# A transformer block on eight cores: a new opening order, later denominator transfers, and GpSimd's Newton steps in pieces

## The chip, the cores and the metric

The kernel runs on all eight cores of one Trainium2 chip. Each core computes one of the eight sequences, with the same instructions, and the cores exchange nothing. Cores 0 to 3 are die 0, cores 4 to 7 die 1, as the profile's list of cores groups them. The metric is the device time of the slowest core in microseconds, us below. Some executions fall into a second, slower state in which one die, sometimes both, shows a lower granted TensorE clock: in the fourth run of the changed kernel cores 4 to 7 show 0.816 to 0.821 and take 3669.6 to 3689.8 us, cores 0 to 3 show 0.985 to 0.99 and take 3208.5 to 3237.1. Such runs are named slow. One execution of each kernel was recorded by the profiler, and its trace gives every core.

TensorE does the matmuls (PE in the profile, PEld for its weight loads), VectorE is DVE, ScalarE is ACT, GpSimd is POOL. SPq is the DMA queue that SyncE issues from. It works in order. On core 5 of the kernel before it issued nothing from 834.4 to 852.80 us, when GpSimd's product `s_ao` had just ended (at 852.77); the store of that product went out then, the load of q behind it at 853.23, and TensorE waited 7.5 us for that q.

## The reference, cut to what matters

```python
h = rms_norm(x, norm1_g) * (1.0 + sc1) + sh1          # x: 4096 x 1024 per core
q, k, v, f_logit, glu_in, gate_logit = split(h @ w_in)
q, k = rms_norm per head of 64 (16 heads)
log_f = log_sigmoid(f_logit + b_forget)
branch_a = forgetting_attention(q, k, v, log_f) @ w_attn_proj      # causal softmax with a decay bias
u = glu_in[..., :1024] * sigmoid(glu_in[..., 1024:])
u = causal_depthwise_conv(u, conv_w, conv_b)                       # 31 taps
branch_b = silu(layer_norm(u)) @ w_conv_proj
merged = sigmoid(gate_a) * branch_a + sigmoid(gate_b) * branch_b
x = x + g1 * (merged @ w_out)
x = x + g2 * (square(relu(h2 @ w_mlp1)) @ w_mlp2)                  # h2: normed and modulated x
```

## The kernel before

The names in the profiles: `s_P` are the exponentials and `p_pS` the scores that they are made of; `s_qT` is a tile of q; `s_dg` are the diagonal matrices of the convolution and `s_us` its tiles of u, read back from the DRAM tensor `ucr`; `s_ysq` are squares for LayerNorm's statistics; `s_Vo` is the scaled V; `s_xn` is a normalised block of x and `s_hT` its transpose.

The kernel has four stages: an opening that computes the modulation and starts the projections (0 to 180 us), the rest of the projections to q, k and v (to about 485 us), attention with the whole convolution branch woven into it (to about 1935 us), and the gates, the output projection and the MLP. A helper records every operation with what it reads and writes, and puts in the waits; inside the engines the order is the order of recording. So the program text decides in which order each engine meets its work.

**Opening.** The modulation row is gathered in `macc` by VectorE. WQ and WK are loaded by GpSimd's queue after it, and name `macc` as something they read, so that WV, which lies on `macc`'s memory, must wait until they have landed:

```python
DMA("pool", WQ[...], wq_d[...], [b_macc], [], d_wq[half], dwrites=[b_WQ[half]])     # both halves, then WK
...
DMA("pool", WV[...], wv_d[...], [], [b_WV[half]], d_wv[half])                       # lies on macc
...
for b in range(4):
    norm1(b)            # ScalarE: sum of squares; VectorE: scale; DVE (b < 4) or GpSimd: shift
    if b >= 1:
        norm2(b - 1)    # TensorE: 8 transposes; ScalarE: copy into hT
norm2(3)
for t in range(NT):     # tiles of 512 rows; tile 0 goes Q, K, V one after another, the others Q K V Q K V ...
    ...
```

**Attention.** 288 groups, each of one key tile of 512 against one query tile of 512 for two heads. A group gives ScalarE four exponentials of 128x1024 and VectorE the scaled V. Half units of the convolution branch are put into the middle of a group, and what is to follow later is put off with `later(us, fn)`, which counts on a clock that the program keeps while it is written: two ticks of 2.2 "model us" for each group, one at its start and one at its end.

```python
def tick(us):                       # run what has come due
    clock[0] += us
    ...
for gi in range(NG + 1):
    tick(2.2)                       # the group's start tick
    ...                             # q_load(i + 2) at the first group of a query tile
    emit_S(gi, 0); emit_exp(gi, 0); emit_S(gi, 1); emit_exp(gi, 1)
    ...                             # half units of the convolution branch
    for p in posts: p()             # their follow-up work: the middle of the group
    posts.clear()
    emit_S(gi, 2); emit_exp(gi, 2); emit_S(gi, 3); emit_exp(gi, 3)
    ...                             # values of the group before, scaled V, masks
    tick(2.2)                       # the group's end tick
```

**The end of a query tile.** The softmax denominators cross the partitions by way of DRAM, in five steps, each put off from the one before:

```python
later(1.5, s0)     # s0: write the sums (Dc -> dscr)
later(6.5, s1)     # s1: read them back reordered (dscr -> dcm), then later(8.5, s2)
# s2 (GpSimd): add, power -1 -> rcm; later(1.0, write rcm -> rscr); later(8.0, s3)
# s3: read back broadcast (rscr -> rb), then later(8.5, s4)
# s4 (GpSimd): ao = Oc * rb; later(1.5, store ao -> aos)
```

**LayerNorm of the convolution branch.** After the second statistics unit of a tile, GpSimd works out the reciprocal root by three Newton steps, thirteen operations in one go, and the eight chunks follow at fixed times:

```python
for it in range(3):
    ...                                                       # four operations of GpSimd
TT(lnM[:], lnM[:], lnY[:], ALU.mult, ..., eng="pool")
for c in range(KC):
    later(18.0 + 4.4 * c, lambda c=c: ln_chunk(t, c))

def ln_chunk(t, c):
    ...                                                       # the STT of an earlier chunk
    TT(z, y, lnY, mult); TT(z, z, lnM, subtract); TS(z, z, g, b)          # VectorE
    act = [lambda: ACT(th, z, Tanh)]                                      # ScalarE
    ...
    later(2.2, lambda: posts.append(mid))                                 # mid() emits the tanh
```

## Time and profile before

Three runs of the kernel before took 3327.37 to 3339.7 us, median 3335.44. The profiled execution took 3332.45 us.

| what | value | where |
|---|---|---|
| span of the eight cores | 3283.4 to 3330.8 us, median 3306 | list of cores |
| start of attention | 481.6 to 489.1 us, median 484.7 | first matmul into p_pS, per core |
| length of attention | 1408 to 1448.5 us, median 1421 | to the first matmul of the stage after it |
| the rest | 1391 to 1400 us | per core |
| TensorE's idle time in attention, core 5 | 1448.0 - 1289.8 = 158 us | windows |

Two lines of this profile were not read closely for the prediction, and they turned out to carry the result. The first is from the list of what each engine waited for, here ScalarE on core 5 in attention. The columns are the engine, what it was about to make and at which line, what it waited for, then total us, times, longest us. `s_lt` is the tanh of LayerNorm, `s_z` its input from VectorE:

```profile
ACT s_lt L363 <- DVE s_z L370: 63.3, 31, 5.7
```

ScalarE stood 63 us, 31 times, before a tanh whose input was not finished. The second view is the timeline of the same core inside one of those times (start, duration, engine, what, and in brackets the idle time before it with what ended it):

```profile
676.30 0.55 DVE L370 TENSOR_SCALAR s_z<-s_z,s_lngc,s_lnbc 128x512 f32<-128x512 f32 x1
...
676.99 0.63 ACT L363 ACTIVATE s_lt<-s_z 128x512 f32<-128x512 f32 x1 [5.72 <-DVE s_z L370]
...
678.01 3.54 ACT L363 ACTIVATE s_P<-p_pS 128x1024 bf16<-128x1024 f32 x4
...
679.17 0.61 PE L348 MATMUL p_pS<-s_qT,s_kT 64*128 64x512 bf16 x2 [3.56 <-ACT s_P L363]
```

ScalarE idles 5.72 us, until VectorE's third operation on z ends at 676.85. The tanh starts 0.14 us later, the exponentials behind it only then, and TensorE waits 3.56 us for one of them to free its scores' buffer. The exponentials had nothing to do with z; they only stood behind the tanh in ScalarE's order, the first of them at 678.01.

### The profile page before, as it was taken

What the parts mean: (1) busy time and instruction counts of PE and PEld (TensorE: products, weight loads), DVE (VectorE), ACT (ScalarE), POOL (GpSimd) and SP (SyncE); (2) the same over time, 40 slices, a digit from 0 to 9 for tenths busy, and PEclk for the clock granted to TensorE, in tenths of its full rate; (3) what the DMA queues carried; (4) which work ended last, traced back from release to release, by engine and by line L of the source; (5) the groups of instructions that cost most, each with busy time, mean ns of one, the idle gap of its engine ahead of it and who ended that gap; (6) DMA issues with size and microseconds to landing.
All of it is one profiled execution on the core that took longest, in us unless ns stands there. A gap on an engine that the chain in (4) does not pass through costs nothing.

```text
span 3330.8 us, 57506 instructions; the slowest of 8 cores (3283.4 to 3330.8 us)
## 1 busy us (share of the span) xinstructions
PE 3062.4 (92%) x23196; PEld 1478.6 (44%) x23196; DVE 1796.6 (54%) x3692; ACT 1654.0 (50%) x2458; POOL 634.3 (19%) x679
## 2 busy tenths in 40 slices
PE   2899989889798988889898999998999999999999
PEld 1455533223232332323333344444666666666666
DVE  5567664474746565473847463664444444444443
ACT  2555557778687777777787821222222222222222
POOL 0212201332323232242424120000001001000000
PEclk8999999999899999999999999999999999999999
DMA  9566457777577868867686654667011111110110
GB/s 222 129 167 164 126 157 140 161 143 162 102 141 137 152 120 134 156 121 164 125 171 142 145 174 129 196 207 244 32 39 52 38 39 39 51 39 33 58 33 26
DMA packets 274757, 400.58 MB, mean 120 GB/s; under 512 B 75829, under 2 KB 205109, under 8 KB 265529
## 3 DMA queue, kind: packets, MB, share of 16 engines
q1 hardware_dynamic: 237658, 275.13, 32.3%
q0 software_dynamic: 36832, 121.76, 19.3%
q8 instruction: 183, 3.00, 0.4%
q14 instruction: 84, 0.69, 0.1%
HBM read 347.80 MB, written 118.31 MB: 140 GB/s over the span
## 4 chain that ended last, share of the span: by engine, by line
PE 68%; DMA 13%; ACT 6%; DVE 6%; SPq 3%; POOL 3%; issue 2%; DVEq 0%; POOLq 0%; ACTq 0%
PE p_po L348 13%; PE p_ph L348 13%; PE p_pC L348 9%; PE p_pF L348 9%; PE p_pmm L348 8%; PE p_pS L348 5%; ACT s_P L363 4%; PE p_pO L348 4%; PE p_pw L348 3%; SPq L344 3%; DMA rscr<-s_rcm 2%; PE p_pD L348 2%; DMA s_dg<-dgs 2%; DMA ucr<-s_u 1%; DMA s_WK<-wk 1%
## 5 line engine op out<-in xcount | busy, mean ns | idle before, releaser
L363 ACT ACTIVATE s_P<-p_pS 128x1024 bf16<-128x1024 f32 (+3 forms) x1152 | 1022.9, 953 | 279.0 <-PE p_pS L348 261.9
L363 ACT ACTIVATE s_rl<-p_ph 128x256 f32<-128x256 f32 x512 | 192.2, 381 | 726.0 <-PE p_ph L348 716.1
L348 PE MATMUL p_pS<-s_qT,s_kT 64*128 64x512 bf16 (+3 forms) x2304 | 382.1, 375 | 112.1 <-ACT s_P L363 91.3
L374 DVE TENSOR_TENSOR s_aT<-s_rl 128x256 bf16<-128x256 f32 x512 | 242.5, 483 | 412.3 <-ACT s_rl L363 392.3
L348 PEld LDWEIGHTS p_pS<-s_qT,s_kT 64*128 64x128 bf16 x2304 | 89.5, 94 | 415.7 <-ACT s_P L363 272.0
L348 PE MATMUL p_pF<-s_hT,s_glw 128*128 128x512 bf16 x1024 | 264.2, 396 | 0.9 <-DVE s_pb L369 0.8
L374 POOL TENSOR_TENSOR s_xl<-s_xl,s_ot 128x512 f32<-128x512 f32 x60 | 79.9, 1341 | 885.6 <-DVE s_ot L374 884.4
L348 PE MATMUL p_pO<-s_P,s_Vo 128*64 128x512 bf16 x1792 | 239.5, 389 | 5.5 <-DVE s_Vo L374 5.3
L363 ACT ACTIVATE s_tha<-p_pC 128x512 f32<-128x512 f32 x128 | 75.5, 596 | 250.8 <-PE p_pC L348 186.0
L348 PE MATMUL p_pF<-s_us,s_dg 128*32 128x512 bf16 x2048 | 138.9, 402 | 23.2 <-DMA s_dg<-dgs 23.2
L374 POOL TENSOR_TENSOR s_ao<-s_Oc,s_rb 128x512 bf16<-128x512 f32 x52 | 67.3, 1295 | 468.2 <-DMA s_rb<-rscr 468.1
L348 PEld LDWEIGHTS p_pF<-s_hT,s_glw 128*128 128x128 bf16 x1024 | 90.2, 101 | 141.5 <-issue 62.9
L384 DVE TENSOR_REDUCE s_ssq<-s_sq 128x8 f32<-128x512 f32 x128 | 84.6, 681 | 115.6 <-ACT s_sq L363 115.6
L348 PEld LDWEIGHTS p_pO<-s_P,s_Vo 128*64 128x64 bf16 x1792 | 83.2, 110 | 132.7 <-issue 44.0
L348 PE MATMUL p_pD<-s_P,s_Wo 128*32 128x512 bf16 x1792 | 138.6, 386 | 0.0
L348 PE MATMUL p_pmm<-s_WQ,s_hT 128*128 128x512 bf16 x512 | 120.6, 391 | 9.7 <-ACT s_hT L363 9.6
L377 DVE SCALAR_TENSOR_TENSOR s_u<-s_th,p_pF 128x512 bf16<-128x512 f32 x64 | 43.8, 684 | 152.3 <-PE p_pF L348 152.2
L348 PE MATMUL p_pF<-s_y,s_wcp 128*128 128x512 bf16 x512 | 124.5, 380 | 0.0
L348 PE MATMUL p_pC<-s_aol,s_wap 128*128 128x512 bf16 x512 | 121.0, 379 | 2.4 <-DVE s_t L377 2.1
L374 DVE TENSOR_TENSOR s_Vd<-s_V,s_Wd 128x256 bf16<-128x256 bf16 (+3 forms) x512 | 121.1, 281 | 2.6
L348 PE MATMUL p_pC<-s_hT,s_wgb 128*128 128x512 bf16 x512 | 121.0, 379 | 0.0
L348 PE MATMUL p_pC<-s_hT,s_wga 128*128 128x512 bf16 x512 | 120.9, 379 | 0.0
(221 smaller groups left out, 5152.6 us busy)
## 6 DMA issues: line engine op xcount, KB each, us to landing
s_us<-ucr SPq DMA_DIRECT2D x256, 135.0 KB, 6.1
s_glw<-wglus POOLq DMA_DIRECT2D x64, 512.0 KB, 8.1
s_x<-x SPq DMA_DIRECT2D x32, 512.0 KB, 9.1
s_hT<-hs POOLq DMA_DIRECT2D x16, 1024.0 KB, 9.6
s_dg<-dgs SPq DMA_DIRECT2D x64, 256.0 KB, 7.7
s_rb<-rscr SPq DMA_DIRECT2D x128, 128.0 KB, 6.7
s_wcp<-wcps POOLq DMA_DIRECT2D x64, 256.0 KB, 7.5
s_wst<-w_ada SPq DMA_DIRECT2D x32, 512.0 KB, 4.3
```

The costliest lines, as they stand in the source:

```text
L344: return P.op(q, lambda e: e.dma_start(out=out, in_=in_), reads=reads, writes=writes, dsem=dsem, dwrites=dwrites)
L348: return P.op("pe", lambda e: e.matmul(out, lhsT=lhsT, rhs=rhs, start=start, stop=stop, skip_group_check=True, **kw), reads=reads, writes= ...
L363: return e.activation(out=out, in_=in_, func=func, **kw)
L374: return P.op(eng, lambda e: e.tensor_tensor(out=out, in0=in0, in1=in1, op=op), reads=reads, writes=writes, dwrites=dwrites)
L377: return P.op("dve", lambda e: e.scalar_tensor_tensor(out=out, in0=in0, scalar=scalar, in1=in1, op0=op0, op1=op1), reads=reads, writes=wri ...
L384: return P.op("dve", lambda e: e.tensor_reduce(out=out, in_=in_, op=ALU.add, axis=AX.X), reads=reads, writes=writes, dwrites=dwrites)
```

## The change

Its intent: start the opening's matmuls earlier and keep GpSimd free there; stop transfers of the denominators from blocking the queue, and GpSimd's LayerNorm run from blocking the denominators. Instructions, bytes and arithmetic stay the same. In the diff, cut to its core:

```diff
-            STT(macc[:], w_t[:], cact[:, kc:kc + 1], macc[:], ..., [b_macc])
+            STT(macc[:], w_t[:], cact[:, kc:kc + 1], macc[:], ..., [b_macc, b_tok] if kc == KC - 1 else [b_macc])
-            DMA("pool", WQ[...], wq_d[...], [b_macc], [], ...)       # WF and WK likewise
+            DMA("pool", WQ[...], wq_d[...], [b_tok], [], ...)
-        hring = arH.ring("hT", 3, [128, KC, 512], BF16, dma=True)
+        hring = Ring([arH.t2("hT%d" % i, [128, KC, 512], BF16, 4) + (P.dsem("hT%d" % i),) for i in range(3)])   # a buffer for each block
 # squares of x blocks 0 and 1 before the modulation is ready; four x loads ahead, not three;
 # the shift of x blocks 1 and 3 goes from VectorE to GpSimd
-        for t in range(NT):
-            for u in range(12):
-                kind, bb = divmod(u, 4) if t == 0 else (u % 3, u // 3)
+        # Q of block 0..3 (first halves, follow-up held), then the held work, second halves,
+        # then Q K V over blocks 0..7 one after another
+        for t in range(2, NT):
+            for u in range(12):
+                kind, bb = u % 3, u // 3
 ...
-                    if c + 3 < KC:                                   # squares made ahead
-                        ysq(t, c + 3)
+                    if c + 4 < KC:
+                        ysq(t, c + 4)
 ...
-                    for it in range(3):
+                    def newton(it):
                         ...                                          # four operations of GpSimd
-                    TT(lnM[:], lnM[:], lnY[:], ALU.mult, ..., eng="pool")
-                    for c in range(KC):
-                        later(18.0 + 4.4 * c, lambda c=c: ln_chunk(t, c))
+                        if it == 2:
+                            TT(lnM[:], lnM[:], lnY[:], ALU.mult, ..., eng="pool")
+                            for c in range(KC):
+                                later(8.0 + 4.4 * c, lambda c=c: ln_chunk(t, c))
+                        else:
+                            later(6.6, lambda: newton(it + 1))
+                    newton(0)
 ...
-                    later(1.0, lambda: DMA("sp", rscr[sl]...))
+                    later(6.0, lambda: DMA("sp", rscr[sl]...))
-                            later(1.5, lambda: DMA("sp", aos[j, :, c, :], ...))
+                            later(8.0, lambda: DMA("sp", aos[j, :, c, :], ...))
-                    later(8.0, s3)
+                    later(18.0, s3)
-            later(6.5, s1)
+            later(11.0, s1)
 ...
-                    if i + 2 < 64:
-                        q_load(i + 2)
+                    if i + 3 < 64:
+                        q_load(i + 3)
```

## The prediction

> **What bounds the kernel now.** I read the cores first, then the busy time by stretch, then what TensorE waited for, then what the DMA queue and GpSimd waited for at the longest of those waits. TensorE is busy 92% of the span of 3330.8 us, and from 2400 us to the end it is busy 923 of 930 us, so it is the engine to follow. The change touches two stretches only: the opening (0 to 180 us) and attention (about 485 to 1935 us).
>
> The opening, from the timeline of TensorE and of GpSimd (columns: start, duration, engine, what, and in brackets the idle time before it with what ended it):
> ```profile
> 39.85 6.47 PE L348 MATMUL p_pmod<-s_macc,s_onesf 128*128 128x512 f32 x8 [39.85 <-DVE s_macc L377]
> 64.10 6.20 PE L348 MATMUL p_pmm<-s_WQ,s_hT 128*128 128x512 bf16 x16 [1.21 <-ACT s_hT L363]
> 70.96 7.07 PE L348 MATMUL p_pmm<-s_WQ,s_hT 128*128 128x512 bf16 x32
> 90.94 1.03 PE L352 MATMUL p_ptx<-s_identb,s_xn 128*128 128x128 bf16 x8 [12.92 <-POOL s_xn L374]
> 91.77 6.05 PE L348 MATMUL p_pmm<-s_WQ,s_hT 128*128 128x512 bf16 x16
> ...
> 86.79 1.74 POOL L344 DMA_DIRECT2D s_WV<-wv  x2 [42.76 <-DMA s_WK<-wk]
> 88.54 2.35 POOL L374 TENSOR_TENSOR s_xn<-s_x,s_shr 128x1024 bf16<-128x1024 f32 x1
> ```
> TensorE stops for 12.9 us because the normalised block 4 comes late; that op of GpSimd stands behind the issue of the V weights, which waits until the K weights have landed. The reason is in the code: the loads of WQ and WK name macc as something they read, and WV lies on macc's memory. Sixteen matmuls take 6.1 us after each stop and half of that (32 in 7.07 us) when TensorE runs on: a stop is paid twice.
>
> Attention, from the list of what TensorE waited for between 480 and 1937 us (total us, times, longest us), then the DMA queue's own list:
> ```profile
> PE p_pS L348 <- ACT s_P L363: 91.3, 145, 3.6
> PE p_pF L348 <- DMA s_dg<-dgs: 23.2, 8, 6.3
> PE p_pS L348 <- DMA s_qT<-qs: 16.9, 3, 7.5
> PE p_pF L348 <- DVE s_ysq L374: 10.2, 7, 2.8
> ...
> SPq L344 <- DMA rscr<-s_rcm: 199.6, 41, 13.9
> SPq L198 <- POOL s_rcm L374: 151.1, 29, 17.7
> SPq L344 <- DMA dscr<-s_Dc: 109.1, 35, 7.2
> SPq L344 <- POOL s_ao L374: 71.4, 15, 18.4
> ```
> The DMA queue stands still for 531 us in these four rows alone, always for the denominator's round trips: write the sums, read them back reordered, write the reciprocals, read them back broadcast, store the result. Each wait at its head delays whatever stands behind it, and eleven times that was a q tile or a conv diagonal that TensorE then waited for: 23.2 + 16.9 = 40.1 us. The longest case, seen in the timelines of GpSimd and of the queue:
> ```profile
> 849.58 1.40 POOL L374 TENSOR_TENSOR s_lnM<-s_lnM,s_lnY 128x512 f32<-128x512 f32 x1
> 851.48 1.29 POOL L374 TENSOR_TENSOR s_ao<-s_Ocx,s_rb 128x512 bf16<-128x512 f32 x1
> ...
> 852.80 0.33 SPq L344 DMA_DIRECT2D aos<-s_ao  x1
> 853.23 0.52 SPq L344 DMA_DIRECT2D s_qT<-qs  x1
> ```
> GpSimd had run Newton steps without a break from about 834 us; the product s_ao came after them, its store stood at the head of the queue, and q behind it. TensorE waited 7.5 us for that q.
>
> The largest row, 91 us for the exponentials, is another matter. It gathers in seven stretches of some 60 us where LayerNorm chunks run: from 660 to 720 us VectorE is busy 51.3 of 60 us and TensorE 45.1, while from 720 to 840 us it is 57 and 117 of 120. There VectorE is full, ScalarE's tanh waits for it, and exponentials wait behind the tanh. The change takes no work off VectorE.
>
> [...] 387 ns for a matmul at 64 us against 221 ns at 71 us, and a granted clock of 0.76 in the 20 us around the q stall at 863 us. [...] each read-back blocks the queue; the trace shows it as the 199.6 and 109.1 us above. [...] the Vd products of 128x256 take 582 ns from 660 to 720 us and 286 ns from 720 to 830 us. [...]
>
> **The change, part by part.**
>
> 1. Opening. WQ, WK and WV load one after another at what the queue can move: the halves of WQ landed at 55.7 and 71.4 us (issue plus 15.2 and 30.0 us), those of WK at 81.2 and 86.3. With the token, WV is issued near 47 us and is here soon after 100 us, as before, but GpSimd is free. TensorE's order becomes Q0 Q1 K0 K1 V0 V1, so V is wanted only after 130 us. The first x blocks are squared before the modulation is ready, so the first transpose can start near 48.5 us, not 52.6, and the first Q matmuls at WQ's landing, 56 us, not 64. Then, however, each block goes transpose, ScalarE copy, eight matmuls in turn: 0.6 to 1.0, 1.4, and 3.1 us cold, so four half blocks last until about 74, when the second half of WQ is there. From then VectorE paces Q: 1.9 us for a half block (the trace's rhythm from 75 to 82 us), 3.9 for a whole one (two reduces, a reciprocal, two products and a copy: 1.27 + 0.25 + 1.29 + 0.68, plus 0.4 of waiting), 1.44 for each block normalised. Four held and four second halves are 8 x 1.9 = 15, five blocks normalised 7, copies 1.4, Q1 16: started at 72, done near 111, and K can start about 3 earlier, at 108. K is 8 x 3.45 + 8 x 0.45 = 31 us, V with its transposes 8 x 3.45 + 3 = 31. Tile 2 then starts near 170 instead of 180.06 us. If VectorE keeps up better than this, TensorE's own work alone would end near 164. I take a gain of 12.
>
> 2. Transfers issued later. Model time is 4.4 us for a group that lasts about 5. The read-back of the sums now follows the write by 9.5 model us (10.7 real) instead of 5, that of the reciprocals by 12 (13.5) instead of 7, the stores wait 8 instead of 1.5 after their product. Median landings are 6 to 8 us, so nearly every such wait should find its data. Together with q three tiles ahead (30 us of lead at the short tiles, where 2 gave 15) and Newton's 17 us cut into pieces of 5 us, the queue does not stand. Of the 40.1 us I take 90%: 36.
>
> 3. The clock behind these stalls: windows 580 to 600 (0.91), 860 to 880 (0.76), 1280 to 1300 and 1400 to 1420 (0.83 each) lose 0.09 + 0.24 + 0.17 + 0.17 of 20 us = 13 us; some of it falls in idle time or would come anyway: 9.
>
> 4. Four squares made ahead instead of three: of 10.2 us about 6, with 2 of clock: 8.
>
> 5. Given back: the q stalls at 863 and 1042 us lie in stretches where VectorE is full, and an earlier TensorE meets exponentials that are not ready: minus 9.
>
> Nothing is added in instructions or bytes, and matmuls, VectorE and ScalarE work are equal. Sum for the slowest core: 12 + 36 + 9 + 8 - 9 = 56 us, which from 3332 leaves 3276. The other cores bound it from below. Core 1 has only 12.8 us of such DMA waits and a span of 3283.4; core 5 has 40.1 and 3330.8. Along that line the waits cost 1.7 us each, with the clock, and a core without any would be at 3262 before the opening and the squares are counted: 3245 after. The slowest of eight, each with some remainder, should lie between the two: 3268.
>
> **The rivals.** (a) VectorE takes over wholly: 40 us of stalls vanish and the row for exponentials grows by as much. For it: VectorE at 17 of 20 us in the LayerNorm stretches. Against: four of the larger stalls (588, 606, 1296, 1411 us, some 21 us together) lie where VectorE is half idle. It would give some 3300. (b) The opening gains nothing, as Q alone is paced by VectorE: 3280. (c) Later reciprocals hold the tiles of O: five buffers, each held 46 model us instead of 31.5, that is 10.5 groups; at the seam of short tiles five are alive at once and the sixth comes 3.5 groups later. If GpSimd is late by more than 17 us there, VectorE stops and everything with it: 3310 or more. (d) LayerNorm starts 3 model us later, and its last Newton piece can stand behind a product that waits for its DMA: VectorE would wait in order for s_lnY, which today it never does. Costs under 10 us if seen. (e) All stalls and all their half clock go on every core, and the opening ends near 164 us: 3245.
>
> **Range and chances.** 3268, within 3242 (case e) to 3298 (case a). The 2% line is 3268.7, so it is nearly even: 0.48 faster, 0.50 within 2%, 0.02 slower.
>
> **What would show it.** Right: no TensorE wait for s_xn from GpSimd in the opening; the first matmuls of tile 2 at 165 to 172 us; the rows for s_dg and s_qT under 5 us together; the queue's waits for rscr, s_rcm, dscr and s_ao under a fifth of 531 us; s_ysq under 5 us; the row for exponentials between 85 and 105 us; cores within 30 us of each other. Wrong: that row above 115 us, VectorE waiting for s_lnY or for the tiles of O, or tile 2 not before 176 us.

## The result, and the profile after

Four runs of the changed kernel took 3232.71, 3238.62, 3237.57 and 3691.32 us; the last is slow. The median is 3238.1 us against 3331.4 us. All ratios in this document are computed as the mean time of one kernel's fast runs over that of the other's of the same rounds, so they are not quite the ratio of the medians. Here the ratio is 0.9715, with a 95% interval of 0.9678 to 0.9752: faster by 2.85%, about 95 us. The predicted 3268 us was 30 us too high, and the measured time lies 4 us below the range.

| profiled executions, both fast | before | after |
|---|---|---|
| span of the eight cores | 3283.4 to 3330.8, median 3306 | 3199.8 to 3231.2, median 3219 |
| start of attention, median | 484.7 | 476.6 |
| length of attention, median | 1421 | 1348 |
| the rest, per core | 1391 to 1400 | 1390 to 1396 |

So 8 us of the gain lie before attention and some 70 in it.

**The opening.** TensorE's timeline on the slowest core, 2:

```profile
58.04 3.59 PE L352 MATMUL p_pmm<-s_WQ,s_hT 128*128 128x512 bf16 x8 [8.62 <-DMA s_WQ<-wq]
...
91.07 1.01 PE L356 MATMUL p_ptx<-s_identb,s_xn 128*128 128x128 bf16 x8 [5.17 <-POOL s_xn L378]
...
177.91 3.62 PE L352 MATMUL p_pmm<-s_WQ,s_hT 128*128 128x512 bf16 x16
```

The matmuls start at 58 us instead of 64, and the one stop of 12.9 us for the normalised block is gone. In its place stand four stops for the same tile, 11.6 us together. Tile 2 starts at 177.9 us, 2.2 us earlier than before. Most of the 8 us are won between tile 2 and attention, where the kernel before has this row on its slowest core (180 to 485 us):

```profile
PE p_pmm L348 <- ACT s_hT L363: 7.2, 6, 1.2
```

In the code, a tile of hT counted as one buffer, so the first matmuls of a tile waited for the copy of its last block. The change gives each block its own. The row is 5.5 to 7.2 us on all cores before and absent on all cores after. It is absent with the opening alone (e3 below) and back at 4.3 to 7.2 us without it (e9).

**Attention.** What TensorE waited for, core 2:

```profile
PE p_pS L352 <- ACT s_P L367: 41.2, 110, 2.0
PE p_pF L352 <- DMA s_dg<-dgs: 14.8, 7, 5.5
PE p_pO L352 <- DVE s_Vo L378: 13.2, 18, 1.9
...
PE p_pF L352 <- DVE s_ysq L378: 4.6, 4, 2.1
```

This is the surprise: the row for exponentials has fallen from 91.3 to 41.2 us, and on all eight cores from 88 to 95 down to 40.6 to 42.0. The prediction had left it between 85 and 105. The rows for q and for the diagonals have gone from 40.1 to 14.8 us, the squares from 10.2 to 4.6; the scaled V has grown from about 5 to 13.2.

ScalarE's own list and timeline, same core:

```profile
ACT s_lt L367 <- DVE s_z L374: 3.5, 5, 1.1
```

```profile
682.89 1.94 ACT L367 ACTIVATE s_P<-p_pS 128x1024 bf16<-128x1024 f32 x2 [0.56 <-PE p_pS L352]
...
683.54 0.55 DVE L374 TENSOR_SCALAR s_z<-s_z,s_lngc,s_lnbc 128x512 f32<-128x512 f32 x1
...
684.72 0.63 ACT L367 ACTIVATE s_lt<-s_z 128x512 f32<-128x512 f32 x1
...
685.24 1.94 ACT L367 ACTIVATE s_P<-p_pS 128x1024 bf16<-128x1024 f32 x2
```

The wait of 63.3 us is 3.5 us now. The third operation on z ends at 684.09, while ScalarE is still busy with two exponentials; the tanh follows them at 684.72 with its input 0.63 us old. Over the first eight chunks of one tile the gap from the end of z to the start of the tanh was 0.14 us and then seven times 0.03 us before, and 0.04 to 1.43 us after. Before seven of those eight tanhs of the kernel before, ScalarE had stood idle, for 0.50 to 5.72 us. Note how small the new gaps still are: the tanh comes a whole group of some 5 us later in ScalarE's order, as shown below, yet its input is at most 1.43 us old. VectorE now finishes z later in relation to that order, so most of the added distance is used up; how little of it would do was not tested.

The windows of the stretch with LayerNorm chunks and of the whole of attention, first before on core 5, then after on core 2 (stretch, its length, busy us with the number of instructions for PE, PEld, DVE, ACT and POOL, granted clock, DMA share, GB/s):

```profile
660.00:720.00 60.00, 45.06 (x495) 16.63 (x496) 51.29 (x112) 41.15 (x55) 26.69 (x28) 0.94 0.70 133
485.00:1933.00 1448.00, 1289.80 (x12095) 447.28 (x12091) 831.43 (x2051) 1084.84 (x1274) 431.18 (x506) 0.96 0.74 143
```

```profile
655.00:715.00 60.00, 54.17 (x572) 19.58 (x572) 51.12 (x129) 50.87 (x64) 16.02 (x18) 1.00 0.69 129
477.00:1835.00 1358.00, 1264.13 (x12096) 443.71 (x12092) 840.50 (x2051) 1084.18 (x1274) 433.65 (x505) 0.99 0.75 152
```

In the LayerNorm stretch VectorE is as busy as before, 51.1 of 60 us against 51.3, and does 129 operations in it instead of 112; TensorE does 54 us instead of 45. So VectorE was not the limit there. Over attention, TensorE's idle time falls from 158 to 94 us. Its busy time falls by another 26 us for the same number of matmuls, with the clock at 0.99 instead of 0.96. In these two traces a low clock goes with stops: after the 7.5 us without q on core 5 of the kernel before, the granted clock was 0.50 from 863.1 to 867 us and 1.00 from 868.5. Cut into windows of 20 us from 485 to 1925 us, the same core shows 0.96 to 1.00 in the 43 windows in which TensorE is busy 18 us or more, and 0.89 in the mean of the 14 in which it is busy less than 16. The changed kernel's core 2, from 477 to 1837 us, has only 3 windows of the second kind and 50 of the first.

The DMA queue, core 2:

```profile
SPq L348 <- DMA ucr<-s_u: 191.9, 39, 10.0
...
SPq L198 <- POOL s_rcm L378: 47.0, 13, 10.1
SPq L348 <- DMA dscr<-s_Dc: 45.5, 11, 9.1
SPq L348 <- DMA rscr<-s_rcm: 30.3, 7, 9.9
```

With 2.6 us for s_ao, which is not shown, the four rows of the prediction come to 125 us here and to 86 to 153 us over the cores, against 531 us before (429 to 531 us). The queue does not run without a stop, though: its wait for `ucr`, the write of u that a read-back follows at once, has grown from 85.5 to 191.9 us. Other rows have grown as well: all of the queue's waits in attention together come to 787 to 841 us per core before and still to 662 to 728 us after. The author's reading, not tested, is that a queue that is less late reaches its next wait earlier. What has changed is how often something that TensorE needs stands behind the wait: eleven waits for q or diagonals, 40.1 us, on core 5 before, and seven, 14.8 us, on core 2 after. e13 below tests the row for `ucr`.

And GpSimd in the middle of Newton steps (s_z and s_lnY are its work tiles there):

```profile
641.09 1.27 POOL L378 TENSOR_TENSOR s_lnY<-s_lnY,s_z 128x512 f32<-128x512 f32 x1
...
642.60 1.67 POOL L378 TENSOR_TENSOR s_rcm<-s_rcm,s_nonec 128x8 f32<-128x8 f32 x1
644.25 1.03 POOL L378 TENSOR_TENSOR s_z<-s_lnY 128x512 f32<-128x512 f32 x1
```

The reciprocals of the denominators now run between two Newton steps.

### The profile page after: what moved, and what is told of

Same layout as the page of the kernel before. It is cut to its first block, busy times and chain, and to the rows that moved or that the text cites. A ratio compares the mean times of both kernels' runs of the same rounds, so it can differ in the third digit from the quotient of the medians.

```text
span 3231.2 us, 57532 instructions; the slowest of 8 cores (3199.8 to 3231.2 us)
## 1 busy us (share of the span) xinstructions
PE 3035.9 (94%) x23196; PEld 1474.9 (46%) x23196; DVE 1802.1 (56%) x3690; ACT 1654.5 (51%) x2458; POOL 642.4 (20%) x681
## 4 chain that ended last, share of the span: by engine, by line
PE 74%; DMA 8%; DVE 7%; ACT 6%; SPq 2%; issue 2%; POOL 1%; DVEq 0%; POOLq 0%; ACTq 0%
PE p_ph L352 13%; PE p_po L352 13%; PE p_pF L352 10%; PE p_pmm L352 9%; PE p_pC L352 9%; PE p_pS L352 6%; PE p_pO L352 5%; ACT s_P L367 4%; PE p_pw L352 3%; PE p_pD L352 3%; SPq L348 2%; DMA s_dg<-dgs 2%; DMA ucr<-s_u 2%; DMA s_wst<-w_ada 1%; DVE s_z L378 1%
## 5 line engine op out<-in xcount | busy, mean ns | idle before, releaser
L352 PE MATMUL p_pS<-s_qT,s_kT 64*128 64x512 bf16 (+3 forms) x2304 | 375.0, 370 | 44.9 <-ACT s_P L367 41.2
L352 PE MATMUL p_pF<-s_hT,s_glw 128*128 128x512 bf16 x1024 | 253.1, 383 | 5.5 <-DVE s_y L373 4.7
L352 PE MATMUL p_pO<-s_P,s_Vo 128*64 128x512 bf16 x1792 | 238.6, 388 | 13.4 <-DVE s_Vo L378 13.2
L352 PE MATMUL p_pF<-s_us,s_dg 128*32 128x512 bf16 x2048 | 134.0, 391 | 14.8 <-DMA s_dg<-dgs 14.8
L388 DVE TENSOR_REDUCE s_ssq<-s_sq 128x8 f32<-128x512 f32 x128 | 85.2, 681 | 91.3 <-ACT s_sq L367 91.0
L378 POOL TENSOR_TENSOR s_xn<-s_x,s_shr 128x1024 bf16<-128x1024 f32 x30 | 70.4, 2348 | 287.2 <-DVE s_x L381 241.5
## 6 DMA issues: line engine op xcount, KB each, us to landing
s_hT<-hs POOLq DMA_DIRECT2D x16, 1024.0 KB, 12.5
```

The source lines that it names most:

```text
L352: return P.op("pe", lambda e: e.matmul(out, lhsT=lhsT, rhs=rhs, start=start, stop=stop, skip_group_check=True, **kw), reads=reads, writes= ...
L378: return P.op(eng, lambda e: e.tensor_tensor(out=out, in0=in0, in1=in1, op=op), reads=reads, writes=writes, dwrites=dwrites)
L388: return P.op("dve", lambda e: e.tensor_reduce(out=out, in_=in_, op=ALU.add, axis=AX.X), reads=reads, writes=writes, dwrites=dwrites)
```

## The experiments

The theory after the result: **the place of the tanh**. In the kernel before, a chunk of LayerNorm is due 18.0 model us after its statistics, and that is the end tick of a group. Its tanh is put off by 2.2, which is the next group's start tick, and it is emitted in the middle of that group: half a group behind VectorE's three operations. In the changed kernel 6.6 + 6.6 + 8.0 makes the chunk due at a start tick; 2.2 later is the end tick of the same group, and the tanh comes in the middle of the next: one and a half groups behind. Nobody asked for this; it falls out of where the numbers land between ticks. The rivals: the exponentials gained because the queue, GpSimd or the opening let VectorE run ahead; or the gain is the queue's after all and the row only shows it.

All kernels named below gave correct results.

### One part at a time

**e1_before_chunk20**: the kernel before with the chunks alone moved to the next tick.

```diff
-                        later(18.0 + 4.4 * c, lambda c=c: ln_chunk(t, c))
+                        later(20.0 + 4.4 * c, lambda c=c: ln_chunk(t, c))
```

> The kernel before with one number changed: the LayerNorm chunks are emitted 20 instead of 18 model us after the statistics, which moves them from the last tick of a group to the first tick of the next and so the tanh of a chunk from half a group to a full group behind its VectorE work. Theory (slot of the tanh): ScalarE's wait for s_z falls from about 60 us to under 8, the wait for the exponentials from 88-95 us to 40-50 on every core, and the time falls by 40 to 55 us with nothing else of the change in place. Rival (the row fell because Newton no longer blocks GpSimd and the DMA queue): both rows stay where they are and the time is within 8 us of before.

Four of its six runs were slow. The two fast ones, 3331.83 and 3301.30 us, give 0.9934 (0.9835 to 1.0032): a gain of 22 us that the interval doesn't separate from nothing. The profile fell in the slow state, with die 0 undisturbed; TensorE's waits on its core 2, in attention:

```profile
PE p_pF L348 <- DMA s_dg<-dgs: 55.3, 15, 11.4
PE p_pS L348 <- ACT s_P L363: 39.5, 105, 2.0
PE p_pS L348 <- DMA s_qT<-qs: 25.9, 5, 10.9
PE p_pO L348 <- DVE s_Vo L374: 19.1, 23, 1.9
```

One number in the program, and the exponentials' row is 39 to 41 us on all cores, as in the changed kernel, with ScalarE's wait for z at 0.7 to 3.4 us. (By the ticks the tanh is now one and a half groups behind, not the full group of the expectation.) So the place of the tanh makes the row. But less time is won than the row gave back: on the cores of die 0 the diagonals now cost 36 to 55 us and q 7 to 26. The queue is the next limit close behind, by these waits. The row for the scaled V rises too, from about 5 us to 14 to 19 on all cores.

The undisturbed dies tell more than the interval. Over the eight undisturbed dies of the six runs the slowest core took 3309 us in the mean, over the twelve of the kernel before in the same rounds 3333 us (standard errors 5 and 3): 24 us less. The gain is there, and about half of the 40 to 55 us expected.

**e2_after_chunk10**: the same the other way, in the changed kernel.

```diff
-                                later(8.0 + 4.4 * c, lambda c=c: ln_chunk(t, c))
+                                later(10.0 + 4.4 * c, lambda c=c: ln_chunk(t, c))
```

> The changed kernel with 8 made 10 in the same place: the chunks go back to the last tick of a group, two model us later, with Newton in pieces and all other parts kept. Theory (slot of the tanh): the wait for s_z comes back to 50-65 us, the exponentials' row to 80-95 us, and the time rises by 35 to 55 us over the changed kernel. Rival (Newton in pieces, or the free queue, did it): rows and time stay within 8 us of the changed kernel.

Two fast runs of four, 3293.05 and 3273.5 us; 0.9834 (0.9756 to 0.9911). The changed kernel loses 0.0119 of the ratio, 40 us, by this number alone. Waits of TensorE and of ScalarE on core 2, from 480 to 1890 us:

```profile
PE p_pS L352 <- ACT s_P L367: 79.6, 136, 3.4
```

```profile
ACT s_lt L367 <- DVE s_z L374: 54.1, 29, 4.0
```

The row is back (78 to 86 us over the cores, each in its whole attention), with ScalarE's wait beside it (49 to 57 us), and the scaled V is down again at 6 to 10 us. What the chunk's later time does besides, by 2.2 model us, is separated from the tanh's place in e7 below.

**e3_before_opening**: the kernel before with the changed opening only.

```diff
 # the hunks of the change up to the projections of tile 2 and later: token, per-block buffers,
 # early squares, held first halves, order Q0 Q1 K0 K1 V0 V1; attention is that of the kernel before
```

> The kernel before with the opening alone of the change (order, per-block buffers, token, early squares); attention as before. Theory: the first attention matmul comes about 8 us earlier on the median core, attention is as long as before (median 1420 us), and the time falls by 6 to 12 us. Rival (the parts multiply: a core that starts attention earlier meets other DMA traffic): attention changes by over 10 us either way.

Three fast runs of five, 3337.08 to 3345.12 us; 1.0007 (0.996 to 1.0053). Attention starts at 469.5 to 480.7 us, median 479, so a few us earlier, and takes 1407 to 1467 us. The interval is 15 us wide to each side and can't show a gain of 8. The waits for q and diagonals were 6 to 49 us per core, median 29, which seemed high; the run of the kernel before further down shows that they vary as much there.

**e4_before_transfers**: the kernel before with the four later times only.

```diff
-                    later(1.0, lambda: DMA("sp", rscr[sl]...))
+                    later(6.0, lambda: DMA("sp", rscr[sl]...))
-                            later(1.5, lambda: DMA("sp", aos...))
+                            later(8.0, lambda: DMA("sp", aos...))
-                    later(8.0, s3)
+                    later(18.0, s3)
-            later(6.5, s1)
+            later(11.0, s1)
```

> The kernel before with the four later issue times of the denominator's transfers alone. Theory: the queue's waits for rscr, s_rcm, dscr and s_ao fall below 250 us from 531, TensorE's waits for s_dg and s_qT together to 5-15 us a core from a median of 18, the exponentials' row stays at 85-95 us, and the time of the slowest core falls by 15 to 30 us. Rival (the queue's waits were the whole cause, the exponentials included): the exponentials' row falls below 60 us and the time by over 50 us.

Four fast runs, 3314.93 to 3325.41 us; 0.9947 (0.9908 to 0.9986): 18 us. The queue's four rows fall to 106 to 135 us per core, and q and diagonals have a median of 15 us (18 in the first profile of the kernel before, 38 in the second), while the exponentials stay at 84 to 90. So later transfers work, alone, for less than the predicted 36 us with their companions, and don't touch the exponentials. The rival that the queue's relief freed ScalarE falls here.

### Two parts together, and the tanh apart from the chunk

**e11_before_chunk20_transfers**: e1 and e4 in one kernel, five numbers of the kernel before.

```diff
 # later(18.0 -> 20.0) for ln_chunk, and the four times of e4
```

> The kernel before with two parts joined that each gave only 0.5 to 0.7% alone: the chunks at 20 model us, and the four later issue times of the denominator's transfers. Theory (two bounds close behind each other, TensorE's wait through the exponentials and the DMA queue; taking one away exposes the other): the exponentials' row 40-45 us, s_dg and s_qT together under 20 us on the median core, and the time 65 to 85 us under before, more than the two single gains together (about 40). Rival (the gains only add): 35 to 45 us.

Four fast runs, 3272.55 to 3284.69 us; 0.9838 (0.9796 to 0.9879), about 54 us. This lies between the two expectations. The two parts alone gave 22 and 18. That together they give more than the sum is not shown, as e1's interval alone is wider than the difference. The row is 40 to 41 us and the queue's four rows 142 to 177 us, but diagonals still cost 21 to 41 us on the cores: the long Newton run is still there.

**e7_after_chunk10_tanh44**: the chunks where e2 has them, and the tanh put off longer, so that it again comes one and a half groups behind.

```diff
-                                later(8.0 + 4.4 * c, lambda c=c: ln_chunk(t, c))
+                                later(10.0 + 4.4 * c, lambda c=c: ln_chunk(t, c))
-            later(2.2, lambda: posts.append(mid))
+            later(4.4, lambda: posts.append(mid))
```

> The changed kernel with the chunks back at the last tick of a group (10 for 8, which cost some 40 us) but the tanh posted 4.4 instead of 2.2 model us after its chunk, so one and a half groups later. Theory (it is the distance of the tanh from its VectorE work, not the place of that work): ScalarE's wait for s_z under 5 us, the exponentials' row at 35-50 us, the time within 12 us of the changed kernel. Rival (the place of the chunk's VectorE work in the group is what counts): the row stays near 82 us and the time 35 us or more above the changed kernel.

Three fast runs of four, 3225.9 to 3237.75 us; 0.9691 (0.9641 to 0.974). The row is 41 to 43 us, ScalarE's wait for z 0 to 1.2. With the chunks at the slow time, the tanh's distance alone brings everything back. So it is the distance between VectorE's z and ScalarE's tanh, not the time of the chunk. Whether it is also a little better than the changed kernel the intervals don't tell.

**e9_after_old_opening**: the changed kernel with the opening of before.

```diff
 # the hunks of the opening undone; attention is that of the changed kernel
```

> The changed kernel with the opening of before. Alone the opening gave nothing. Theory (its 8 us were swallowed in attention because the queue bounded there; in the changed kernel the queue is free): the first attention matmul 8 us later than in the changed kernel, attention as long, time 5 to 12 us above the changed kernel. Rival (the opening is worth nothing in either): within 3 us.

Three of five runs were slow, and no interval was made of the two fast ones, 3252.06 and 3249.55 us. Their mean over that of the kernel before in the same rounds is 3250.8 / 3339.4 = 0.9735, 7 us worse than the changed kernel. Attention starts at 481 to 489 us and takes 1339 to 1368 us, as long as in the changed kernel within its spread (1333 to 1360). So in these traces the opening's part is its earlier end; two fast runs cannot show more.

**e8_after_late_dg**: two new ideas on top of the changed kernel. TensorE stops once for 12.8 us near the start of the MLP, for a relu of ScalarE, and after it the granted clock is 0.50 from 2234.7 to 2240 us, 0.95 in the 5 us after that and then 1.00. The code suggests why: six late weight loads name a buffer of VectorE's squares as read, so that VectorE may not write it again until they have landed, and the relu's buffers fill up. It is the same false chain as macc's in the opening, and the same token should undo it. And the diagonal is issued ahead of the four u loads of the same convolution unit.

```diff
+        b_late = Buf()
-                    TT(a_t[:], r_t[:], r_t[:], ALU.mult, [r_b], [a_b])
+                    TT(a_t[:], r_t[:], r_t[:], ALU.mult, [r_b], [a_b, b_late] if tt == 0 and f == 3 else [a_b])
-                        late.append(a_b)
+                        late.append(b_late)
+            DMA("sp", d_t[:]..., dgs[c], ...)      # before the loop of four u loads, not after it
```

> The changed kernel with two small repairs: the loads of the last MLP weights read a token instead of the activation tile (the same repair as the opening's; today the tile's next writer waits until the loads have landed and TensorE stops for 12.8 us), and a conv diagonal is loaded ahead of the four pieces of u that must wait for their own round trip. Theory: the 12.8 us stop goes with its half clock, s_dg falls from 1-20 us to under 5 but some moves to s_us; 12 to 22 us under the changed kernel, near 3220. Rival (the stop is the weights' own landing): the stop stays, now named by the weights, and the time is within 5 us of the changed kernel.

Three fast runs of four, 3223.84 to 3234.51 us; 0.9683 (0.9635 to 0.9732), 11 us better than the changed kernel with overlapping intervals. The stop of 12.8 us is 0.9, and the part after attention takes 1381 us instead of 1394. The diagonals wait 0 us, but the u tiles behind them wait 3 to 19 us instead: that part only moved the wait.

### The remaining parts, taken out of the changed kernel

**e10_after_whole_newton**: Newton in one go again, with the chunks at the tick that keeps the tanh's place.

```diff
-                    def newton(it):                      # pieces, 6.6 apart, chunks at 8.0
+                    for it in range(3):
                         ...
+                    for c in range(KC):
+                        later(20.0 + 4.4 * c, lambda c=c: ln_chunk(t, c))
```

> The changed kernel with Newton's thirteen steps in one piece again, the chunks kept at the first tick of a group (20 model us). Two parts of before joined (chunks and transfers) had still shown 21 to 41 us of waits for s_dg and 1 to 13 for s_qT a core. Theory (the unbroken Newton holds GpSimd 17 us and with it the reciprocals and the queue; the pieces remove this): s_dg back to 15-30 us on the median core, exponentials' row still 40-45, time 12 to 30 us above the changed kernel. Rival (q three tiles ahead and the squares made the difference): s_dg under 12 us on the median core, time within 6 us of the changed kernel.

Four fast runs of five, 3265.9 to 3268.7 us; 0.9796 (0.9747 to 0.9846). The pieces are worth 0.0081 of the ratio, 27 us. TensorE's waits on core 2:

```profile
PE p_pF L352 <- DMA s_dg<-dgs: 43.4, 10, 10.7
```

Diagonals wait 17 to 43 us per core, against 1 to 20, and no other row of TensorE's grew, the one for exponentials being 39 to 42 us: the cost shows in the diagonals, by way of the queue.

**e12_after_q2_ysq3**: q two tiles ahead and three squares ahead, as before.

```diff
-                    if i + 3 < 64:            # q_load
+                    if i + 2 < 64:
-                    if c + 4 < KC:            # ysq
+                    if c + 3 < KC:
```

> The changed kernel with q two tiles ahead and three squares made ahead, as before. Theory (the q part is hidden once the queue is free, the squares cost 5 us): s_qT under 5 us a core, s_ysq back to about 10 us from 5, time 4 to 12 us above the changed kernel. Rival (q three ahead carries the gain in the queue): s_qT over 8 us on the median core and the time 15 to 30 us above.

Three fast runs of four, 3238.34 to 3254.56 us; 0.9741 (0.9671 to 0.981): 9 us, less than the intervals. In the trace the squares' row is 10 to 13 us instead of 5, and q waits 0 to 4.6 us instead of 0.

**e13_best**: an attempt to beat both kernels: e7, the token of e8, and the convolution's loads put off from 11.0 to 13.2 so that the queue need not stand for `ucr`.

```diff
 # e7, the token of e8, and
-                    later(11.0, lambda: conv_load(n))
+                    later(13.2, lambda: conv_load(n))
```

> A version meant to beat both: the changed kernel with the tanh one and a half groups behind its chunk (10 and 4.4), the token for the late MLP weights, and the conv loads asked for at 13.2 instead of 11 model us, so that they stand less at the head of the queue for their own round trip. If the conv loads are better later: the queue's wait for ucr falls from about 200 us to under 150, s_dg and s_us together stay under 15 us a core, time 12 to 25 us under the changed kernel. If they come too late: s_us or s_dg over 25 us a core and the time at or above the changed kernel.

Three fast runs of four, 3225.57 to 3244.64 us; 0.9709 (0.9619 to 0.9799). The queue's wait for `ucr` falls from about 200 to 73 to 76 us on the three cores looked at, and nothing is won: diagonals wait 8 to 21 us now, since their loads are issued later (0 to 15 us in e15 below, which differs by this number alone). Some 125 us less of standing bought no time in this run; the author reads from it that a queue that stands costs only what comes too late behind it.

**before_again**: the kernel before once more, to see how its waits vary.

```diff
 # no change
```

> The kernel before, profiled once more on the chip of these runs, for the spread of its stages: attention starts at 481 to 490 us on every core, the exponentials' row 85-95 us, s_dg and s_qT together 10 to 45 us a core with a median near 20. If instead the median is over 30, the cores' DMA waits in the opening's run on its own (25 to 49 us on five cores) say nothing about the opening.

One run, 3356.75 us. Attention starts at 478 to 490 us; the exponentials' row is 86 to 94; q and diagonals wait 14.5 to 59.4 us per core, median 38. In the first profile the core with the largest such wait had 40.1. So these waits vary from run to run, the median over the cores from 18 to 38 us, and the waits of e3 say nothing against its opening. It also means that the 40.1 us that the prediction set out to save were one core's draw from such a spread.

### The last question, and the best version

Two things were open: how much the later transfers are worth with the rest in place, and whether e13 without its delayed loads is the best version.

**e14_after_old_transfers**: the changed kernel with the four old times.

```diff
 # the four times of e4, the other way
```

> The changed kernel with the four issue times of the denominator's transfers as before. Theory (with TensorE no longer held by the exponentials, the queue is the bound, and the early issue makes it stand for every round trip): s_dg and s_qT together 20-45 us a core, exponentials' row still 40-45, time 25 to 50 us above the changed kernel, more than the 18 us that the later times gave alone. Rival (Newton in pieces and the slot of the tanh are all there is): waits under 15 us, time within 8 us of the changed kernel.

Four fast runs, 3245.58 to 3283.64 us; 0.9797 (0.9715 to 0.9878): the later times are worth 0.0082, 27 us, though this interval overlaps that of the changed kernel. The queue and VectorE on core 0:

```profile
SPq L348 <- DMA rscr<-s_rcm: 191.1, 41, 13.6
SPq L198 <- POOL s_rcm L378: 122.6, 34, 8.5
```

```profile
DVE s_z L378 <- POOL s_lnY L378: 16.6, 2, 15.4
```

The four rows are 435 to 485 us again, but q waits 0 us and diagonals 12.5 to 27.6 us. The exponentials' row stays at 40 to 42. The second view is a cost that does not come by way of the queue: VectorE waits for GpSimd's last Newton result, 2.3 to 16.6 us per core, and the row for the scaled V is 14 to 33 us against 13 to 20 in the changed kernel. This is the mechanism of the prediction's rival (d). How the 27 us divide between the two ways is not shown.

**e15_tanh_late**: e7 and the token of e8.

```diff
 # ln_chunk 8.0 -> 10.0, tanh 2.2 -> 4.4, and the token b_late
```

> The changed kernel with two repairs joined: the tanh one and a half groups behind its chunk (alone about 5 us better than the changed kernel) and the token for the late MLP weights (took a 13 us stop away). If they add: 3220 us or a little under, ratio to before 0.963 to 0.968. If not: 0.969 or more.

Three of five runs were slow. The two fast ones took 3210.98 and 3209.0 us, the fastest of all kernels here: 3210.0 / 3330.9 = 0.9637, without an interval. In the profiled run all cores lie between 3184.7 and 3209.4 us, with the exponentials' row at 42 to 43 us, diagonals at 0 to 15 and the rest after attention at about 1381. It beats both kernels, by some 121 and 26 us. The undisturbed dies agree: over all five runs the slowest core of each of these seven dies took 3200 to 3209 us, against 3218 to 3237 us for the seven of the changed kernel.

### The ledger

Each part taken out of the changed kernel, as the difference of the ratios times 3335 us; the last column is an estimate of its 95% range, from the root of the summed squares of both ratios' intervals:

| part taken out | run | loss | range |
|---|---|---|---|
| the tanh's place | e2 | 40 us | 11 to 68 |
| Newton in pieces | e10 | 27 us | 6 to 48 |
| later transfers | e14 | 27 us | -3 to 57 |
| q three ahead, four squares | e12 | 9 us | -18 to 35 |
| opening | e9 | 7 us | two runs, none |

The sum, 110 us, is more than the 95 us won. The parts are not independent: with one bound gone, the next one, close behind, decides how much is won, as e1 shows, where the exponentials' row falls from 88 to 95 us to 39 to 41, and diagonals, now 36 to 55 us on the cores of die 0, take part of the time back.

## Why the prediction was wrong, point by point

**The step that failed** is the paragraph "The largest row, 91 us for the exponentials, is another matter", which concluded "There VectorE is full, ScalarE's tanh waits for it, and exponentials wait behind the tanh. The change takes no work off VectorE." The chain in it is right, and the trace shows each link. The conclusion is not: VectorE at 51 of 60 us is no bound, as it does the same 51 of 60 after, with more work done per time. What made exponentials wait was that the tanh stood in ScalarE's order just half a group behind the operations that feed it. The change moves it by a whole group without touching VectorE. Its worth is 40 us by e2 (11 to 68), and e7 shows that it is the distance; the sum lacked the term altogether. The other parts of the ledger come to 70 us, near the 64 us that the prediction forecast in all, so the missing term is about as large as the 30 us by which the number was off. Rival (d) came within reach of it: it noted that LayerNorm starts 3 model us later, but looked only for a cost, and never asked at which tick the tanh then lands.

**1. Opening, 12 us.** Right in direction and too large. Q starts at 58 us as worked out (56), but "no TensorE wait for s_xn from GpSimd" was wrong: four waits, 11.6 us together, for blocks 4 to 7. GpSimd is free, as predicted; it stands idle itself before each of these blocks, 1.6 to 8.9 us, until VectorE's product `s_x` is ready. K starts at 115.9 us instead of 108 and tile 2 at 177.9 instead of 170, past the 176 us that were named as a sign of failure. Attention starts 8 us earlier all the same, for a reason that the prediction did not name: some 6 us of it are the waits for `s_hT` after tile 2. So its 12 is near the 8 partly by luck. e9 puts the opening at about 7.

**2. Transfers, 36 us.** The mechanism is shown by e4, e10 and e14: later times and pieces unload the queue, and TensorE waits less for what stands behind. The size was probably too small: the times are worth 27 and the pieces 27, each with the other in place, though in the kernel before the times alone gave only 18 (e4). q waits 0 as predicted, but diagonals wait 0.8 to 19.5 us over the cores, so "under 5 us together" fails on most of them, and the four rows are 86 to 153 us where a fifth of 531 is 106. "The queue does not stand" was wrong: in all its rows it stands 662 to 728 us.

**3. Clock, 9 us.** Under-counted. Over attention the same matmuls take 26 us less of busy time between the two cores compared. Over the same time the granted clock is 0.99 instead of 0.96 and TensorE idles 94 us instead of 158; all stops count in that, those for exponentials too, and it can't be divided among the parts.

**4. Squares, 8 us.** The mechanism is right: the row is 4.6 to 5.6 us on all cores (over the 5 named on three of them), and e12 doubles it; the worth, 9 us with q, is within the intervals.

**5. Given back, 9 us.** The guess was that exponentials would take it. They took nothing. Something else did take about as much: the row for the scaled V rose from about 5 to 13 to 20 us. It comes with the tanh's place: e1 moves that alone and has 14 to 19 us, e2 moves it back and has 6 to 10.

**The rivals.** (a) and (b) did not come: the row fell, and the opening gained. (c) No hold on the tiles of O was seen. (d) came, but small: VectorE waits for s_lnY and s_lnM 3.1 us on the slowest core and 2.4 on one other, and with the old times of e14 4.6 to 20.1 us. (e), 3245 us, was nearest, for a reason that it did not contain; by the prediction's own sum it should read 3262 - 12 - 8 = 3242. The spread of the cores, 31.4 us, is just over the 30 named.

**One reading to correct.** The 582 ns for the Vd products is a mean of six, of which one took 2.06 us and the other five, worked out from the two figures, 0.29 us in the mean, as later. So it is one slow operation, from 671.80 to 673.86 us, while GpSimd's product `s_ao` ran from 672.40 to 673.69, and not a stretch of slow products. No term of the sum rested on it.

**What stays open.** The worth of the opening alone (e3) lies inside its interval. By which path the tanh's later place makes TensorE wait more for the scaled V was not tested, nor how e14's loss divides between the queue and GpSimd.

## What to carry to other kernels

When a row says that an engine waits for a result, look at two things before calling the producer full: whether it is busy all the time, and how far behind the producer the consumer stands in its own engine's order. Here a tanh that stood half a group behind its input in ScalarE's order held up the exponentials behind it: ScalarE stood 63.3 us for z and TensorE 91.3 us for exponentials, against 3.5 and 41.2 with one and a half groups. Putting it one group later cost little, some 10 us more of waiting for the scaled V against some 50 us less for the exponentials. And where emission times are rounded to ticks, a shift that looks like a small delay can move an operation across half a group: replay the ticks for each thing that the change moves.

A queue of transfers is to be read the same way. Here it stood 429 to 531 us in four rows of round trips, and giving each pair of transfers more time was worth 27 us (e14, -3 to 57). How long it stands does not tell by itself: in all rows together it still stood 662 to 728 us in the changed kernel, against 787 to 841 before.
